# Half of a head's weight transposes go from TensorE to VectorE and DMA, with round-robin buffers and a larger DMA reserve in the order

## The chip, the cores and the metric

The kernel runs on one core of one Trainium2 chip. The core has TensorE (matmuls, PE in the profile), VectorE (DVE), ScalarE (ACT), GpSimd (POOL) and SyncE (SP), whose queue issues every DMA of this kernel. The metric is the device time of one execution in microseconds. Before the change, three runs took 823.62, 824.11 and 825.51 us; the median is 824.11.

## The reference, cut to what matters

One layer of an encoder is computed for a prompt of 1024 positions and a sample of 32 later positions, 1056 rows of 1024 features, in float32. Eight heads of 64 features ("A") do a banded softmax attention with a bias by relative position, eight heads ("B") a stick-breaking attention over all earlier positions.

```python
hn = rmsnorm(h, g_pre)
qa, ka, va, ga, qb, kb, vb, gb = split(hn @ w_in)          # 8 x 512 columns
# A: each chunk of 64 rows reads its own chunk and the 8 before
w = softmax(qa @ ka.T * HD ** -0.5 + bias[rel] , where ok); oa = w @ va
# B: strictly causal
z = qb @ kb.T * HD ** -0.5
w = exp(log_sigmoid(z) + sum of log_sigmoid(-z) over later keys); ob = w @ vb
y = concat(oa * silu(ga), ob * silu(gb)) @ w_out
h = h + rmsnorm(y, g_post)
h = h + sigmoid(h @ w_ple_gate) * (p @ w_ple)
```

The keys and values of both kinds of heads are returned too.

## The kernel before, in words

Every float32 operand of a product is split into a high part, rounded to the format of TensorE's fast float32 product, and the rest (hi and lo); a product is then two or three matmuls.

The work comes in three parts. First x is normalized, transposed and split (tiles `hnh`, `hnl`), while `w_ple` is applied to the first rows. Then come eight pairs of heads, A0, B0, A1, B1 and so on to B3. For each pair the projections of q, k and v (`mm_qA`, `mm_kA`, `mm_vA`, 72 matmuls of 352 columns each) run between the attention of the pair before; with the last pair run the eight gates. Last come the output product and the gate product by a scheme of seven products instead of eight (`o`, `g`).

The attention of one head goes over eight tiles of 128 queries (`attention`, L711). `scores(i)` (L728) makes the scores of tile i: two matmuls into a bank `S`, and for A a VectorE operation that adds the bias and finds the maximum, an exponential on ScalarE into `w1` (tile `be`), a reciprocal, and a scaling on POOL. For B it is two sigmoids on ScalarE, a scan on VectorE and a product on POOL. `weights_t(i)` (L771) then turns the weights: TensorE transposes each block of 128 keys into a bank `ptw`, ScalarE copies the bank into the high part `wTh`, and VectorE subtracts it from the bank for the low part `wTl`. `values(g)` (L798) multiplies the turned weights of four tiles (g = 0 or 1) with V into `PV`, and the head's output goes to DRAM. A tile of A has at most five blocks of keys: 1, 2, 3, 4, 5, 5, 5, 5 for i = 0 to 7. Tile i's transposes are called two tiles behind its scores, and the value products two behind the last tile.

V itself is turned in another way already (`values_out`, L611): VectorE transposes 32 x 32 squares, a DMA writes the result to DRAM (`swapA`), and four DMAs read it back with the squares in their places (`stv`).

The order of all this isn't the order of the calls. The calls only record operations (`Recorder`); `order` (L307) then plans them with a cost for each operation (`cost`, L274) and an order of keys (attention before projections), engine by engine, and issues them so. Each engine, and SP's queue, takes its own list in order. A DMA is taken to land 1500 ns after its issue, plus its bytes at 320 B/ns, plus a reserve `DMA_MARGIN` (L165) of 800 ns. The planner has no cost for ScalarE's table loads.

Buffers have a fixed number of rooms by tag: `om` and `be` (softmax and sigmoid work, and at the start the rows of x and their squares) have three rooms of a full row each; `wTh` and `wTl` have two rooms each of four blocks by 512 queries. A new tile waits for the tile that had the room before.

`g_pre` is spread over 128 partitions by a matmul of a row of ones, one partition deep (L1218 and the lines behind it). The 32 sample rows of V are kept in a tile `vsT`, filled by POOL (`after_v`, L697) and read by `sample_attention` (L840).

Of the kernel before, what the change touches and what calls it, by code (L numbers as in the profile page):

```python
# [13 lines left out]
P = 128  # L14
# [12 lines left out]
NT = 9  # L27

# [127 lines left out]

class Op:
# [7 lines left out]
DMA_NS, DMA_RATE, DMA_MARGIN = 1500, 320.0, 800  # L165
# [3 lines left out]
class Pool:  # L169
# [8 lines left out]
    def tile(self, shape, dtype, tag=None, name=None, bufs=1):  # L178
        b = Buf(shape, dtype, self, tag or name, name, bufs)
        line = self.tags.setdefault(b.tag, [])  # L180
        after = {line[-1].place} if line else {self.opened} if self.opened else set()
        b.place = self.rec.node("CTL", b.take, (), {}, after)
        if len(line) >= bufs:
            self.rec.turns.append((b.place, line[len(line) - bufs]))
        self.ops.append(b.place)
        line.append(b)
        return b
# [12 lines left out]
class Recorder:  # L200
# [43 lines left out]
    def add(self, eng, what, args, kw):  # L244
        writes, reads = [], []
        method = what[1] if isinstance(what, tuple) else ""
        for i, a in enumerate(args):
            if isinstance(a, (View, Raw)):
                (writes if i == 0 or (method == "tensor_tensor_reduce" and i == 7) else reads).append(a)
        for k, a in kw.items():  # L250
            if isinstance(a, (View, Raw)):
                (writes if k in ("out", "accum_out") else reads).append(a)
        o = self.node(eng, what, args, kw, set())
        for mine, write in ((reads, False), (writes, True)):
            for v in mine:
                b = v.buf
                hit = False
                for other, box, wrote in b.uses:
                    if other is not o and (write or wrote) and all(p < y and x < q for (p, q), (x, y) in zip(v.box, box)):
                        o.after.add(other)  # L260
                        hit = True
                if b.pool is not None:
                    if not hit:
                        o.after.add(b.place)
                    b.pool.ops.append(o)
                b.uses.append((o, v.box, write))
        o.busy, o.late = self.cost(eng, method, args, kw, writes, reads)
        o.shared = eng == "POOL"
        if eng == "DVE":
            sbuf = [v for v in reads if isinstance(v, View) and not v.buf.psum and v.free() > 4]  # L270
            o.shared = len(sbuf) > 1 or (method == "tensor_copy" and len(sbuf) == 1 and not writes[0].buf.psum)

    @staticmethod
    def cost(eng, method, args, kw, writes, reads):  # L274
# [3 lines left out]
        psum = any(isinstance(v, View) and v.buf.psum for v in reads)  # L278
# [96 lines left out]
    def emit(self, tc):  # L375
        ops = self.order()
        with tc.manual_schedule():
            for o in ops:
                if o.eng == "CTL":
                    o.what()  # L380
                    continue
                args = [a.get() if isinstance(a, (View, Raw)) else a for a in o.args]
                kw = {k: a.get() if isinstance(a, (View, Raw)) else a for k, a in o.kw.items()}
                if isinstance(o.what, tuple):
                    getattr(getattr(tc.nc, o.what[0]), o.what[1])(*args, **kw)  # L385
                else:
                    o.what(*args)
# [3 lines left out]
def stream_step(  # L391
# [26 lines left out]
    r_dr = scratch([8, 768], "r_dr")  # L418
    ple_dr = scratch([T, D], "ple_dr")
# [25 lines left out]
    vsT = const.tile([NS, 4, P], F32, tag="vsT", name="vsT")  # L445
# [29 lines left out]
    def ensure(j):  # L475
# [6 lines left out]
        if j == 2:  # L482
            pair = [at.tile([P, 2, 4, P], F32R, tag=tag, name=f"{tag}_{kind}{p}", bufs=2) for tag in ("wTh", "wTl")]
# [14 lines left out]
    def load_x(t):  # L498
        n = min(P, T - t * P)
        if t == 3:  # L500
            x34.append(at.tile([P, 2, D], F32, tag="wTh", name="x34", bufs=2))
        xt = x34[0][:, t - 3] if t in (3, 4) else at.tile([P, D], F32, tag="om", name=f"x{t}", bufs=3)
# [9 lines left out]
    def scale_x(t, xt, n, gp):  # L512
        sq = at.tile([P, D], F32, tag="be", name=f"sq{t}", bufs=3)
# [25 lines left out]
    def bias_rows():  # L539

        rb = at.tile([8, 257], F32, tag="om", name="rb", bufs=3)
        dma(rb, rel_bias[0])
        R = at.tile([8, 768], F32, tag="be", name="R", bufs=3)
# [101 lines left out]
    def col_steps(j):  # L645
# [65 lines left out]
    def attention(ab, p, h):  # L711
# [16 lines left out]
        def scores(i):  # L728
# [5 lines left out]
            w0 = at.tile([P, SEQ + 1], F32, tag="om", name=f"om{nm}_{i}", bufs=3)  # L734
            w1 = at.tile([P, SEQ], F32, tag="be", name=f"be{nm}_{i}", bufs=3)
# [31 lines left out]
            state[i] = w1  # L767

        wT = {}

        def weights_t(i):  # L771
            g, q = i // 4, (i % 4) * P
            for j in range(i // 4 + 1):
                if (g, j) not in wT:
                    wT[g, j] = [at.tile([P, 4, 4 * P], F32R, tag=tag, name=f"{tag}{nm}_{g}_{j}", bufs=2) for tag in ("wTh", "wTl")]
            b0 = lo_block(i)
            w1 = state.pop(i)
            b = b0
            while b <= i:
                j = b // 4  # L780
                e = min(i + 1, 4 * (j + 1))
                m = e - b
                pt = psum("T", f"ptw{nm}_{i}_{j}")
                for x in range(m):
                    nc.tensor.transpose(pt[:, x * P:(x + 1) * P], w1[:, (b - b0 + x) * P:(b - b0 + x + 1) * P], ident)
                hi, lo = wT[g, j]
                o = b - 4 * j
                src = pt[:, 0:m * P].rearrange("p (b c) -> p b c", b=m)
                nc.scalar.copy(hi[:, o:o + m, q:q + P], src)
                nc.vector.tensor_tensor(lo[:, o:o + m, q:q + P], src, f(hi[:, o:o + m, q:q + P]), ALU.subtract)  # L790
                b = e
# [6 lines left out]
        def values(g):  # L798
# [41 lines left out]
    def sample_attention(ab, gi):  # L840
# [9 lines left out]
        def load():  # L850
            Kc = at.tile([P, 4, 256], F32, tag="be", name="Kc" + nm, bufs=3)
# [34 lines left out]
        def scores():  # L886
# [6 lines left out]
            w0 = at.tile([P, SEQ + 1], F32, tag="om", name="w0" + nm, bufs=3)  # L893
            w1 = at.tile([P, SEQ], F32, tag="be", name="w1" + nm, bufs=3)
# [22 lines left out]
            Vc = at.tile([P, 4, 256], F32, tag="be", name="Vc" + nm, bufs=3)  # L917
            dma(Vc, cv[0, 0, :, h4, :].rearrange("(b p) h d -> p b (h d)", p=P))
            bx["Vc"] = Vc

        def weights():
# [24 lines left out]
            for a in range(2):  # L946
                new, c = vsT[:, at_[a], :], slice(a * P, (a + 1) * P)
                nc.vector.tensor_copy(vh4[0:NS, c], new)
                nc.vector.tensor_tensor(vl4[0:NS, c], new, f(vh4[0:NS, c]), ALU.subtract)
# [273 lines left out]
    nc.vector.tensor_copy(ghl[:, 0], grow)  # L1223
    nc.vector.tensor_tensor(ghl[:, 1], grow, f(ghl[:, 0]), ALU.subtract)
# [513 lines left out]
```

## Time and profile before

| | |
|---|---|
| median of 3 runs | 824.11 us |
| the profiled execution | 822.94 us |
| its span, first to last instruction | 821.2 us |
| TensorE, matmuls busy | 806.5 us |
| VectorE busy | 588.7 us |
| ScalarE busy | 536.5 us |
| POOL busy | 498.6 us |
| moved by DMA | 135.57 MB |

The profile is one execution with every instruction's start and length. Names are out<-in by the program's tiles, with the numbers of buffers left out and the pair left out, so `wThA<-ptwA` is the copy of turned weights of any head of A. Every operation is issued from one line of the recorder (L385), so groups are told apart by tile. A row of the groups has the busy time of the group, the mean length of one in ns, and the idle time of the engine before them with what ended it. Matmuls are pipelined: the busy time counts a matmul to its modelled end, and the next has begun by then.

### The profile page before, as it was taken

What the parts mean: (1) busy time and instruction counts of PE and PEld (TensorE: products, weight loads), DVE (VectorE), ACT (ScalarE), POOL (GpSimd) and SP (SyncE); (2) the same over time, 40 slices, a digit from 0 to 9 for tenths busy, and PEclk for the clock granted to TensorE, in tenths of its full rate; (3) what the DMA queues carried; (4) which work ended last, traced back from release to release, by engine and by line L of the source; (5) the groups of instructions that cost most, each with busy time, mean ns of one, the idle gap of its engine ahead of it and who ended that gap; (6) DMA issues with size and microseconds to landing.
All of it is one profiled execution on the core that took longest, in us unless ns stands there. A gap on an engine that the chain in (4) does not pass through costs nothing.

```text
span 821.2 us, 14722 instructions
## 1 busy us (share of the span) xinstructions
PE 806.5 (98%) x4814; PEld 742.7 (90%) x4814; DVE 588.7 (72%) x1165; ACT 536.5 (65%) x1179; POOL 498.6 (61%) x559
## 2 busy tenths in 40 slices
PE   9999999999999999999999999999999999999997
PEld 7999999999999998999999998999998787888786
DVE  5717588987687898687887787983664676686755
ACT  4735588776476667687685676653437866886741
POOL 5625785996676959554753454675462527599613
PEclk9999999999999999999999999999999999999999
DMA  8419854526764545633413544253489847749733
GB/s 296 122 39 277 208 178 149 142 60 203 214 178 155 152 135 153 154 91 88 97 40 98 139 122 145 74 160 112 134 264 291 293 142 242 252 153 361 248 117 128
DMA packets 137855, 135.57 MB, mean 165 GB/s; under 512 B 36450, under 2 KB 103818, under 8 KB 137779
## 3 DMA queue, kind: packets, MB, share of 16 engines
q1 hardware_dynamic: 137778, 134.64, 55.0%
q8 instruction: 38, 0.62, 0.3%
q14 instruction: 39, 0.31, 0.2%
HBM read 85.41 MB, written 40.79 MB: 154 GB/s over the span
## 4 chain that ended last, share of the span: by engine, by line
PE 83%; DVE 6%; ACT 4%; DMA 4%; issue 2%; SPq 0%; POOL 0%; DVEq 0%; ACTq 0%
PE mm_gB L385 5%; PE mm_qA L385 5%; PE mm_kB L385 5%; PE mm_kA L385 5%; PE mm_vA L385 4%; PE mm_vB L385 4%; PE mm_qB L385 4%; PE PVB L385 4%; PE SB L385 3%; PE ple L385 3%; PE PVA L385 3%; PE mm_gA L385 3%; PE ptwB L385 3%; PE ptwA L385 3%; PE SA L385 3%; PE g1P L385 2%
## 5 line engine op out<-in xcount | busy, mean ns | idle before, releaser
L385 POOL TENSOR_TENSOR beB<-beB,omB 128x128 f32<-128x128 f32 (+7 forms) x64 | 87.2, 1364 | 75.3 <-ACT beB L385 31.5
L385 DVE TENSOR_TENSOR_SCAN omB<-omB 128x128 f32<-128x128 f32 (+7 forms) x64 | 106.5, 1675 | 6.6 <-POOL omB L385 3.5
L385 POOL TENSOR_SCALAR beA<-beA,statA 128x640 f32<-128x640 f32 (+2 forms) x64 | 48.2, 755 | 50.1 <-DVE statA L385 47.9
L385 DVE TENSOR_TENSOR wTlA<-ptwA,wThA 128x128 fp32r<-128x128 f32 (+3 forms) x96 | 45.5, 483 | 27.8 <-ACT wThA L385 27.0
L385 ACT CAST wThA<-ptwA 128x128 fp32r<-128x128 f32 (+3 forms) x96 | 39.7, 422 | 32.1 <-PE ptwA L385 30.5
L385 ACT ACTIVATE omB<-SB 128x384 f32<-128x384 f32 (+5 forms) x96 | 47.1, 501 | 14.7 <-DVE SB L385 8.3
L385 DVE TENSOR_TENSOR wTlB<-ptwB,wThB 128x512 fp32r<-128x512 f32 (+3 forms) x96 | 50.7, 545 | 8.1 <-ACT wThB L385 7.2
L385 ACT CAST wThB<-ptwB 128x512 fp32r<-128x512 f32 (+3 forms) x96 | 44.7, 485 | 16.9 <-PE ptwB L385 16.3
L385 ACT ACTIVATE beA<-omA,statA 128x640 f32<-128x640 f32 (+2 forms) x64 | 44.7, 700 | 7.2 <-DVE statA L385 5.6
L385 ACT ACTIVATE beB<-SB 128x384 f32<-128x384 f32 (+5 forms) x96 | 45.4, 500 | 6.0 <-PE ptwB L385 3.2
L385 PE MATMUL ptwB<-ident,beB 128*128 128x128 f32 x288 | 44.9, 274 | 0.1
L385 PE MATMUL ptwA<-ident,beA 128*128 128x128 f32 x240 | 40.2, 274 | 0.8 <-POOL beA L385 0.8
L385 PEld LDWEIGHTS ptwB<-ident,beB 128*128 128x128 f32 x288 | 34.9, 140 | 3.4 <-DVE wTlB L385 0.8
L385 POOL TENSOR_TENSOR gB<-gB,gB 128x256 f32<-128x256 f32 x32 | 29.1, 929 | 13.8 <-issue 7.4
L385 PE MATMUL SB<-kdB,LB 128*128 128x384 f32 (+5 forms) x96 | 34.6, 364 | 0.3 <-ACT beB L385 0.2
L385 POOL TENSOR_TENSOR oB<-oB,oB 128x256 f32<-128x256 f32 x32 | 28.4, 903 | 8.6 <-DMA oB<-in_w_out_dram 4.6
L385 PE MATMUL SB<-klB,LB 128*128 128x384 f32 (+5 forms) x96 | 33.1, 346 | 0.0
L385 DVE CUSTOM_DVE_ANT_0 omA<-SA,biasA 128x320 f32<-128x320 f32 (+2 forms) x64 | 30.7, 479 | 3.2 <-PE SA L385 1.9
L385 PEld LDWEIGHTS ptwA<-ident,beA 128*128 128x128 f32 x240 | 30.2, 140 | 2.7 <-POOL beA L385 1.1
L385 PE MATMUL SA<-kdA,LA 128*128 128x320 f32 (+2 forms) x96 | 30.5, 327 | 1.4 <-DVE LA L385 1.2
L385 PE MATMUL SA<-klA,LA 128*128 128x320 f32 (+2 forms) x96 | 29.9, 321 | 0.0
L385 POOL TENSOR_TENSOR h<-h,x 128x512 f32<-128x512 f32 (+1 forms) x18 | 23.3, 1321 | 0.8 <-DVE h L385 0.8
(712 smaller groups left out, 2674.5 us busy)
## 6 DMA issues: line engine op xcount, KB each, us to landing
x<-in_x_prompt_dram SPq DMA_DIRECT2D x8, 512.0 KB, 5.9
oB<-in_w_out_dram SPq DMA_DIRECT2D x16, 256.0 KB, 4.0
sum_dro<-oB SPq DMA_DIRECT2D x16, 256.0 KB, 2.3
gB<-in_w_ple_gate_dram SPq DMA_DIRECT2D x16, 256.0 KB, 3.8
sum_drg<-gB SPq DMA_DIRECT2D x16, 256.0 KB, 2.8
x<-in_x_prompt_dram SPq DMA_DIRECT2D x16, 256.0 KB, 3.7
h_dr<-h SPq DMA_DIRECT2D x8, 512.0 KB, 3.5
ht<-h_dr SPq DMA_DIRECT2D x8, 512.0 KB, 5.5
```

Of the source, the lines that this page charges most:

```text
L385: getattr(getattr(tc.nc, o.what[0]), o.what[1])(*args, **kw)
```

## The change

There are five parts.

1. The turning of the weights of A's tiles 0, 2, 4 and 6 (`swapped`). VectorE transposes 32 x 32 squares of `w1` into the tile's other work tile `w0`, grouped by target; a DMA writes `w0` to DRAM, four DMAs (one for each 32 partitions) read it back into `w1`, ScalarE copies `w1` into the high part and VectorE subtracts the high part from `w1` for the low part. TensorE and the bank `ptw` aren't used for these tiles. The other tiles of A and all of B stay on TensorE, now in groups of four blocks from the tile's first block.
2. Round-robin rooms (`Arena`): `om`, `be`, `wTh` and `wTl` are one tile each, of 3076, 3384, 4224 and 4224 columns, from which pieces of the size needed are handed out in turn, starting over at the end; a piece waits for all pieces that lay where it lies. The turned weights lie one query tile behind the other, and the value product reads them through an access pattern with a step (`Segments`).
3. The planner's reserve on a DMA's landing is 2000 ns instead of 800.
4. `g_pre`: the ones are 128 x 128 and the row stands in the first of 128 rows, the others cleared by VectorE.
5. The sample's rows of V go by DMA to DRAM and come back with the cached values, in place of the copies on POOL.

```diff
+def swapped(ab, p, h, i):
+    return ab == "A" and i % 2 == 0
...
-DMA_NS, DMA_RATE, DMA_MARGIN = 1500, 320.0, 800
+DMA_NS, DMA_RATE, DMA_MARGIN = 1500, 320.0, 2000
...
+class Segments:
+    def __init__(self, buf, start, step, n):
+        self.buf, self.start, self.step, self.n = buf, start, step, n
...
+    def get(self):
+        base = self.buf.get()[:, self.start:self.start + P]
+        return bass.AP(tensor=base.tensor, offset=base.offset, ap=[base.ap[0], [self.step, self.n], [1, P]])
...
+class Arena:
...
+    def tile(self, shape, name, dtype=None):
...
+        size = -(-n // 8) * 8
+        if self.at + size > self.cols:
+            self.at = 0
+        lo, hi = self.at, self.at + size
+        self.at = hi
...
+        for c, d, x in self.live:
+            if c < hi and lo < d:
+                old.append(x)
...
+        b.place = self.rec.node("CTL", take, (), {}, {self.whole.place} | {x.place for x in old})
+        for x in old:
+            self.rec.turns.append((b.place, x))
...
+    ring0, ring1 = Arena(rec, at, "om", 3076), Arena(rec, at, "be", 3384)
+    ringh, ringl = (Arena(rec, at, x, 33 * P, F32R) for x in ("wTh", "wTl"))
...
-            nc.gpsimd.tensor_scalar(vsT[:, slot(ab, p), :], tok[0:NS, 8, :], 1.0, 1.0, ALU.mult, ALU.mult)
+            dma(vs_dr[ab][:, p * P:(p + 1) * P], tok[0:NS, 8, :])
...
-            w0 = at.tile([P, SEQ + 1], F32, tag="om", name=f"om{nm}_{i}", bufs=3)
-            w1 = at.tile([P, SEQ], F32, tag="be", name=f"be{nm}_{i}", bufs=3)
+            w0 = ring0.tile([P, n + (ab == "B")], f"om{nm}_{i}")
+            w1 = ring1.tile([P, n], f"be{nm}_{i}")
...
+        LAID = {("A", 0): (3, 13), ("A", 1): (4, 20), ("B", 0): (3, 13), ("B", 1): (7, 29)}
...
+            if swapped(ab, p, h, i):
+                nc.vector.transpose(w0[:, 0:n * P].rearrange("p (c b q) -> p b c q", c=4, q=32), w1)
+                dr = scratch([P, n * P], f"swap{nm}_{i}")
+                dma(dr, w0[:, 0:n * P])
+                for c in range(4):
+                    x = dr[:, c * n * 32:(c + 1) * n * 32].rearrange("(g k) x -> k g x", k=32)
+                    dma(w1[32 * c:32 * c + 32].rearrange("k (g x) -> k g x", g=4), x)
+                src = w1.rearrange("p (g b q) -> p g b q", g=4, q=32)
+                hi, lo = (x.rearrange("p (b g q) -> p g b q", g=4, q=32) for x in (hi, lo))
+                nc.scalar.copy(hi, src)
+                nc.vector.tensor_tensor(lo, src, f(hi), ALU.subtract)
+                return
+            for b in range(0, n, 4):
...
+                nc.scalar.copy(hi[:, c], pt[:, 0:m * P])
+                nc.vector.tensor_tensor(lo[:, c], pt[:, 0:m * P], f(hi[:, c]), ALU.subtract)
...
-                nc.tensor.matmul(acc[:, c], v2[:, b, :], wT[g, j][half][:, b - 4 * j, c], start=(n == 0), stop=(n == len(todo) - 1))
+                step = LAID[ab, g][0]
+                w = Segments(wT[g][half], c.start * step + b * P, step * P, (c.stop - c.start) // P)
+                nc.tensor.matmul(acc[:, c], v2[:, b, :], w, start=(n == 0), stop=(n == len(todo) - 1))
...
-    ones = at.tile([1, P], F32R, tag="ot", name="ones", bufs=3)
+    ones = at.tile([P, P], F32R, tag="ot", name="ones", bufs=3)
...
-    ghl = at.tile([1, 2, D], F32R, tag="wTl", name="ghl", bufs=2)
+    ghl = ringl.tile([P, 2, D], "ghl")
+    for part in range(2):
+        nc.vector.memset(f(ghl[:, part]), 0.0)
```

More of the change, by code (lines that the diff above doesn't have):

```diff
@@ L269, in add @@
         if eng == "DVE":
-            sbuf = [v for v in reads if isinstance(v, View) and not v.buf.psum and v.free() > 4]
+            sbuf = [v for v in reads if isinstance(v, (View, Segments)) and not v.buf.psum and v.free() > 4]
             o.shared = len(sbuf) > 1 or (method == "tensor_copy" and len(sbuf) == 1 and not writes[0].buf.psum)
@@ L277, in cost @@
         n = out.free() if isinstance(out, View) else 1
-        psum = any(isinstance(v, View) and v.buf.psum for v in reads)
+        psum = any(isinstance(v, (View, Segments)) and v.buf.psum for v in reads)
         if eng == "PE":
@@ L482, in ensure @@
         if j == 2:
-            pair = [at.tile([P, 2, 4, P], F32R, tag=tag, name=f"{tag}_{kind}{p}", bufs=2) for tag in ("wTh", "wTl")]
+            pair = [ringl.tile([P, 2, 4, P], f"w{x}_{kind}{p}") for x in "hl"]
         for kh in range(2):
@@ L766, in scores @@
                 nc.gpsimd.tensor_scalar(w1[:, 0:n], w1[:, 0:n], m[:, 3:4], 1.0, ALU.mult, ALU.mult)
-            state[i] = w1
+            state[i] = w0, w1
         wT = {}
+        LAID = {("A", 0): (3, 13), ("A", 1): (4, 20), ("B", 0): (3, 13), ("B", 1): (7, 29)}
         def weights_t(i):
[L772 to L775, printed above, removed]
+            g = i // 4
+            step, size = LAID[ab, g]
+            if g not in wT:
+                wT[g] = [x.tile([P, size * P], f"{x.name}{nm}_{g}") for x in (ringh, ringl)]
@@ L776, in weights_t @@
             b0 = lo_block(i)
[L777 to L783, printed above, removed]
-                for x in range(m):
[L785 to L791, printed above, removed]
+            w0, w1 = state.pop(i)
```

79 lines of the change are left out of this document (58 added, 21 removed).

## The prediction

> **What bounds the kernel.** I read the page's busy shares first, then its chain, then what TensorE waited for, and last the stretches in which the heads of A run.
>
> ```profile
> span 821.2 us, 14722 instructions
> PE 806.5 (98%) x4814; PEld 742.7 (90%) x4814; DVE 588.7 (72%) x1165; ACT 536.5 (65%) x1179; POOL 498.6 (61%) x559
> PE 83%; DVE 6%; ACT 4%; DMA 4%; issue 2%; SPq 0%; POOL 0%; DVEq 0%; ACTq 0%
> ```
> ```profile
> PE PVB L385 <- DVE v2B L385: 1.8, 1, 1.8
> ...
> PE PVA L385 <- ACT wThA L385: 1.2, 1, 1.2
> ...
> PE ptwA L385 <- POOL beA L385: 0.8, 1, 0.8
> ...
> PE PVA L385 <- DVE v2A L385: 0.6, 1, 0.6
> ```
>
> TensorE is busy for 98% of the span and makes up 83% of the chain. The second fence is TensorE's list of waits behind its first microseconds (total, times, longest): no wait reaches 2 us. So work taken from TensorE shortens the kernel unless it comes back as a wait. The question is whether the order, fixed at build time, still always has a matmul ready.
>
> ```profile
> core 0: us, PE busy (x) PEld busy (x) DVE busy (x) ACT busy (x) POOL busy (x), PEclk, DMA share, GB/s
> 64.00:124.00 60.00, 57.32 (x375) 55.09 (x374) 43.75 (x125) 40.25 (x95) 41.40 (x53) 1.00 0.80 219
> ...
> 185.00:248.00 63.00, 61.61 (x406) 59.22 (x406) 47.16 (x143) 40.18 (x98) 44.13 (x59) 1.00 0.69 196
> 248.00:312.00 64.00, 63.48 (x418) 61.16 (x417) 55.87 (x88) 45.48 (x105) 46.03 (x51) 1.00 0.50 145
> 312.00:368.00 56.00, 55.38 (x362) 52.69 (x361) 40.92 (x124) 41.21 (x98) 37.66 (x43) 1.00 0.51 136
> ...
> 435.00:492.00 57.00, 56.81 (x384) 55.17 (x383) 44.14 (x140) 39.38 (x95) 25.13 (x33) 1.00 0.49 128
> ```
>
> These are the four stretches of the A pairs (64, 185, 312 and 435 us) and one B pair (248 us). VectorE is at 73 to 79% in the A stretches and at 87% in the B stretch, where TensorE still works 63.48 of 64 us. Hence VectorE at 87% is not yet a bound. The first A stretch also has the DMA engines at 0.80.
>
> **The transposes that go.** Tiles 0, 2, 4 and 6 of a head of A have 1, 3, 5 and 5 blocks of keys, 14 for a head and 112 for eight heads, of the 240 below. The built order agrees: 4814 matmuls become 4702.
>
> ```profile
> 330.30 0.49 PE L385 MATMUL mm_kB<-hnl,wh_kB 128*128 128x352 f32 x2
> 330.63 0.60 PE L385 MATMUL ptwA<-ident,beA 128*128 128x128 f32 x4
> 330.98 0.41 PE L385 MATMUL mm_kB<-hnl,wh_kB 128*128 128x352 f32 x1
> 331.23 0.22 PE L385 MATMUL SA<-kdA,LA 128*128 128x128 f32 x1
> ```
> ```profile
> L385 PE MATMUL ptwA<-ident,beA 128*128 128x128 f32 x240 | 40.2, 274 | 0.8 <-POOL beA L385 0.8
> ```
>
> In the timeline (start, length) two projections take 0.33 us, 0.165 each. Four transposes take 0.35, and the projection behind them takes 0.25 instead of 0.165. That is 0.44 for four, 0.11 each, and 112 x 0.11 = 12.3 us. The bounds are 112 x 0.35/4 = 9.8 (no delay behind them) and 112 x 40.2/240 = 18.8 (the group's busy time, which includes drains that overlap other matmuls). I take 12.3, because matmul starts measure what follows and busy time doesn't.
>
> **What takes their place.** A swapped tile costs one square transpose on VectorE, one DMA out, four DMAs back, one ScalarE copy and one VectorE subtraction, both now from SBUF.
>
> ```profile
> L385 DVE STREAM_TRANSPOSE vxA<-stvA 128x1024 f32<-128x1024 f32 x4 | 5.0, 1240 | 0.4 <-ACT stvA L385 0.4
> ...
> L385 DVE STREAM_TRANSPOSE ktA<-stkA 128x512 f32<-128x512 f32 x4 | 2.8, 703 | 11.8 <-ACT stkA L385 11.8
> ```
> ```profile
> L385 DVE TENSOR_TENSOR wTlA<-ptwA,wThA 128x512 fp32r<-128x512 f32 x24 | 16.5, 688 | 10.9 <-ACT wThA L385 10.6
> ...
> L385 DVE TENSOR_TENSOR oT<-woT,oT 128x512 fp32r<-128x512 f32 x8 | 7.6, 966 | 1.2 <-ACT oT L385 1.2
> ...
> L385 DVE TENSOR_TENSOR oB<-woB,oB 128x512 fp32r<-128x512 f32 x8 | 6.8, 854 | 7.0 <-ACT oB L385 7.0
> ...
> L385 DVE TENSOR_TENSOR wTlA<-ptwA,wThA 128x128 fp32r<-128x128 f32 x24 | 6.7, 279 | 0.2
> ```
>
> The two square transposes give 166 ns + 1.05 ns a column, so 0.30, 0.57, 0.84 and 0.84 us for a head: 20.4 us for eight. The subtraction from PSUM goes from 279 (128 columns) to 688 (512); with both inputs in SBUF, 512 columns take 854 to 966, some 1.32 times as long. Six subtractions a head (half of the 45.5 us of the whole group) become four: (0.28 + 0.55 + 0.82 + 0.82) x 1.32 x 8 = 26 against 22.7 us. VectorE gains about 24 us, 6 for each A pair: the 64 us stretch goes from 43.75 to some 50 of 60, 83%, still below the B stretch. I cost it at nothing; without that cover it is bounded by 24 us. ScalarE's copies change from six to four a head, by one us or two in all. On POOL eight small copies of V go.
>
> ```profile
> swapA<-vxA SPq DMA_DIRECT2D x4, 512.0 KB, 2.6
> stvA<-swapA SPq DMA_DIRECT2D x16, 128.0 KB, 3.4
> ...
> o_dr<-otA SPq DMA_DIRECT2D x32, 64.0 KB, 2.2
> ...
> out_dram<-ktA SPq DMA_DIRECT2D x16, 64.0 KB, 3.2
> ```
> ```profile
> L385 SPq DMA_DIRECT2D stvA<-swapA x16: 303/423/464, 78.3 to 438.5; - x16
> ...
> DMA to landing us min/median/max: 2.6/3.4/7.0
> ```
>
> SP's queue gets 160 DMAs for the tiles and 12 for V of the sample (608 become 780). At 0.42 us an issue that is 72 us over 440, and it lies beside TensorE. Each tile crosses two landings in a row: 2.6 + 3.4, four issues, a copy and a subtraction, about 9 us from square to operand. Everything behind a swap in SP's queue stands when the queue waits for the square or for the first landing: weight loads, output rows, the doubled keys. The data is 1792 columns x 128 x 4 B = 0.92 MB each way for a head, 3.67 MB a pair, 61 GB/s in a stretch. In the first A stretch 219 + 61 = 280 stands against 219/0.80 = 274 GB/s: 2% of 60 us, between 0 and 1.3 us; I take 0.7. The other stretches have room.
>
> **Waits that the new order brings.** I counted in both built orders, behind the first 60 us, the places where TensorE has no matmul left between the start of a producer on another engine and the matmul that needs it. There are 13 before and 38 after; 13 of the 38 are value products of A that stand directly behind the copy of a swapped tile. The four waits listed above, 1.8 + 1.2 + 0.8 + 0.6 = 4.4 us, are what such places cost before, 0.34 each. The 25 new ones cost between 0 and 25 x 0.34 = 8.5 us. I take the middle, 4.2: the planner now reserves 1.5 + 1.0 + 2.0 us for 320 KB out, while 512 KB landed in 2.6, so half of these producers should be early.
>
> ```profile
> 117.25 0.75 ACT L385 CAST wThA<-ptwA 128x384 fp32r<-128x384 f32 x2
> 118.02 1.28 ACT L385 ACT_TABLE_LOAD   x1
> 119.31 0.28 ACT L385 ACTIVATE omB<-SB 128x128 f32<-128x128 f32 x1
> ```
> ```profile
> 313.90:317.90 4.00, 3.44 (x20) 1.00 0.40 90
> ...
> sum 28.00, PE 27.13; mean PE 3.88
> ```
>
> ScalarE's table loads go from 8 to 18 in the built order: where A hands over to B, late exponentials of A now stand between early sigmoids of B, and the planner's costs have no term for it. Ten loads x 1.28 = 12.8 us of ScalarE. The second fence is TensorE in the four microseconds behind each of the seven old loads between heads: it lost 0.87 us in all. So ten more cost 1.2 us by that rate, 12.8 if all lies on the path; I take 1.5, because they come in pairs. [...]
>
> **The rest.** The rooms change which tile waits for which; no row prices that, and it is counted in the 25 places. The reserve moves consumers of every DMA later in the order; that can take away waits such as the 1.8 us on v2B, which stands behind a DMA round trip, so its gain is bounded by 1.8 + 0.6.
>
> ```profile
> 0.87 0.38 DVE L385 MEMSET newh<- 128x384 f32 x1 [0.87 <-PEq L1726]
> ...
> 2.18 0.81 DVE L385 CAST ghl<-grow 1x1024 fp32r<-1x1024 f32 x1 [0.93 <-DMA grow<-in_g_pre_dram]
> ...
> 3.02 1.21 DVE L385 TENSOR_TENSOR ghl<-grow,ghl 1x1024 fp32r<-1x1024 f32 x1
> ...
> 5.92 2.07 PE L385 MATMUL gpre<-ghl,ones 1*128 1x512 f32 x4
> ```
>
> g_pre on 128 rows adds two clears of 1024 columns, 0.38 x 1024/384 = 1.0 us each, ahead of the copy: 1.25 + 2.0 + 0.81 + 1.21 = 5.3 us, before the matmul at 5.92. It costs nothing.
>
> **Sum.** The profiled execution took 822.94 us, 1.2 below the median 824.11. 822.94 - 12.3 + 4.2 + 1.5 + 0.7 = 817.0, and on the median's scale 818.2: I predict 818.
>
> **The rivals.**
> - Everything is covered. The swapped tiles are early everywhere, the loads hide, and late landings of V stop: 824.1 - 12.3 - 2 = 810. For it: 0.87 us lost behind seven loads; against it: 13 value products with nothing in front of them.
> - The chain of a swapped tile comes late, and TensorE, which takes its queue in order, stands at A's value products. It decides from 12.3/13 = 0.95 us each. The 1.8 us on v2B is just such a square with a DMA round trip; at 1.8 each, 824.1 - 12.3 + 23.4 = 835. For it speaks a landing of 7.0 us among medians of 3.4, and that 64 KB in packets of 128 B (ktA) took 3.2 us where packets of 1 KB (otA) took 2.2: the swapped reads have packets of 128 to 640 B. [...]
> - ScalarE's loads fall on the path at the hand-overs: 824.1 - 12.3 + 12.8 + 4.2 = 829. Against it: the old loads.
> - The change doesn't do what it says: the attention chain sets the pace and the freed 12.3 us turn into idle TensorE. 822.5 to 825.8. Against it: the shares of the other engines.
>
> **Chances.** 818 (812.5 to 822.4) has 0.45, all covered 0.15, late chains 0.22, loads on the path 0.10, no change 0.08. A measurement tells 0.2%, 1.6 us, from no change. So faster has 0.60, same 0.08, slower 0.32. For 8 in 10 the range reaches from 809 (12.3 and the late landings gone, and a little more busy time than starts show) to 832, which takes in the loads and most late chains.
>
> **What would show it.** ptwA x128 and about 27 us busy; TensorE busy near 794; 48 square transposes, of which 32 near 0.3 to 0.84 us; 18 table loads. The four stretches of A shorter by 2 to 3 us each shows the sum right. In TensorE's waits, PVA behind ACT wTh in more than ten places of under 0.5 us shows the 4.2 right; over 0.95 us, the second rival. If waits sit at the hand-overs behind loads, it is the third. The forecast is wrong if SP's queue makes the weights late, which would show as projections waiting for wh or wl.

## The result and the profile after

The changed kernel takes 830.10 us (median of 13 runs, 825.94 to 831.01), the kernel before 823.17 us in runs beside it (13 runs, 819.42 to 826.20). The ratio is 1.0079 with a 95% interval of 1.0059 to 1.0098. By the ratio it is 6.5 us slower, where 6 us faster was predicted. The profiled execution took 828.38 us.

The busy shares and the chain of the page of the changed kernel:

```profile
span 826.4 us, 14790 instructions
PE 796.8 (96%) x4702; PEld 729.9 (88%) x4702; DVE 604.0 (73%) x1175; ACT 547.6 (66%) x1173; POOL 506.6 (61%) x551
PE 73%; DMA 9%; ACT 6%; POOL 4%; SPq 3%; DVE 3%; issue 2%; ACTq 0%; POOLq 0%; DVEq 0%
```

TensorE works 9.7 us less than before, and the span is 5.2 us longer. Its idle time has doubled, from 821.2 - 806.5 = 14.7 to 826.4 - 796.8 = 29.6 us. In the chain TensorE falls from 83 to 73%; DMA comes to 9% from 4, and SP's queue, nothing before, to 3%.

The same five stretches by the clock (start and end, length, busy time and count for each engine, granted clock, DMA share, GB/s):

```profile
64.00:124.00 60.00, 55.06 (x344) 51.81 (x343) 44.56 (x124) 40.62 (x87) 35.66 (x46) 1.00 0.86 244
185.00:248.00 63.00, 58.40 (x371) 55.78 (x370) 46.06 (x131) 37.27 (x84) 34.31 (x43) 0.97 0.76 212
248.00:312.00 64.00, 62.45 (x408) 59.95 (x407) 57.59 (x92) 51.13 (x114) 47.55 (x57) 1.00 0.59 166
312.00:368.00 56.00, 53.61 (x346) 51.32 (x345) 42.43 (x128) 35.82 (x81) 38.20 (x46) 1.00 0.74 194
435.00:492.00 57.00, 54.87 (x356) 52.49 (x354) 42.87 (x131) 36.02 (x79) 23.05 (x28) 1.00 0.55 145
```

Most of the loss is in the four A stretches: TensorE is idle there for 14.1 of 236 us, where it was 4.9 before, which is 9.2 of the 14.9 us of added idle time. VectorE is hardly fuller in the first two (44.56 and 46.06, before 43.75 and 47.16), because the work moves slower. In the second stretch the granted clock was 0.97.

TensorE's waits in the changed kernel (total, times, longest):

```profile
PE PVA L453 <- ACT wTh L453: 3.5, 5, 1.1
PE PVsA L453 <- DVE Vh0sA L453: 3.5, 1, 3.5
PE ptwA L453 <- POOL be L453: 3.2, 3, 1.7
PE SB L453 <- ACT be L453: 1.9, 2, 1.7
PE SA L453 <- DVE statA L453: 1.7, 2, 0.9
...
PE mm_vB L453 <- ACT wh_vB L453: 0.3, 1, 0.3
```

Value products behind the copy of a weight tile are there, as feared. But none of the four next to them is at a swapped tile's operands; the longest single one is the sample's attention, which waits for cached values (`Vh0sA`) that come by a DMA of their own.

The moved work, in groups (count, busy time, mean ns, idle before and what ended it) and as DMA issues (count, KB each, median us to landing):

```profile
L453 PE MATMUL ptwA<-ident,be 128*128 128x128 f32 x128 | 21.5, 282 | 3.9 <-POOL be L453 3.2 <-POOL om L453 0.6
L453 DVE STREAM_TRANSPOSE om<-be 128x640 f32<-128x640 f32 x16 | 13.4, 839 | 1.7 <-POOL be L453 1.4
L453 ACT CAST wTh<-be 128x640 fp32r<-128x640 f32 x16 | 11.7, 730 | 11.1 <-DMA be<-swapA 11.1
L453 DVE TENSOR_TENSOR wTl<-be,wTh 128x640 fp32r<-128x640 f32 x16 | 14.6, 920 | 3.2 <-ACT wTh L453 3.1
L453 ACT ACT_TABLE_LOAD x18 | 23.1, 1283 | 3.5 <-issue 1.3 <-DVE statA L453 1.2 <-PEq L1815 0.7
swapA<-om SPq DMA_DIRECT2D x16, 320.0 KB, 4.1
be<-swapA SPq DMA_DIRECT2D x64, 80.0 KB, 2.8
DMA packets 161470, 150.52 MB, mean 182 GB/s; under 512 B 47393, under 2 KB 125385, under 8 KB 161394
```

The instructions are as forecast: 112 transposes gone, square transposes of 0.84 us, 18 table loads. The 128 transposes left are busy for 21.5 us and not for the 27 forecast: that figure took the 12.3 us, which are counted by starts, off the 40.2 us of busy time. New is that ScalarE stands 11.1 us before the copies of the large swapped tiles, waiting for their landing.

### The profile page after: what moved, and what is told of

It reads as the page before. It is cut to its first block, busy times and chain, and to the rows that moved or that the text cites. A ratio compares the mean times of both kernels' runs of the same rounds, so it can differ in the third digit from the quotient of the medians.

```text
span 826.4 us, 14790 instructions
## 1 busy us (share of the span) xinstructions
PE 796.8 (96%) x4702; PEld 729.9 (88%) x4702; DVE 604.0 (73%) x1175; ACT 547.6 (66%) x1173; POOL 506.6 (61%) x551
## 4 chain that ended last, share of the span: by engine, by line
PE 73%; DMA 9%; ACT 6%; POOL 4%; SPq 3%; DVE 3%; issue 2%; ACTq 0%; POOLq 0%; DVEq 0%
PE mm_gB L453 5%; PE mm_qA L453 5%; PE mm_vA L453 5%; PE mm_gA L453 4%; PE mm_kB L453 4%; PE PVB L453 4%; PE ptwB L453 4%; PE mm_kA L453 4%; SPq L453 3%; PE SB L453 3%; PE mm_qB L453 3%; PE g0P L453 2%; PE g1P L453 2%; PE o1P L453 2%; PE o3P L453 2%; PE o0P L453 2%
## 5 line engine op out<-in xcount | busy, mean ns | idle before, releaser
L453 POOL TENSOR_TENSOR be<-be,om 128x256 f32<-128x256 f32 (+8 forms) x66 | 91.2, 1391 | 48.9 <-DVE om L453 22.6
L453 DVE TENSOR_TENSOR_SCAN om<-om 128x256 f32<-128x256 f32 (+8 forms) x66 | 110.8, 1688 | 4.5 <-ACT om L453 3.7
L453 POOL TENSOR_SCALAR be<-be,statA 128x640 f32<-128x640 f32 (+2 forms) x64 | 47.1, 741 | 67.1 <-DVE statA L453 38.3
L453 ACT CAST wTh<-ptwB 128x512 fp32r<-128x512 f32 (+3 forms) x96 | 44.1, 484 | 22.7 <-PE ptwB L453 21.4
L453 ACT ACTIVATE be<-om,statA 128x640 f32<-128x640 f32 (+3 forms) x64 | 44.5, 696 | 18.4 <-DVE statA L453 14.6
L453 DVE TENSOR_TENSOR wTl<-ptwB,wTh 128x512 fp32r<-128x512 f32 (+3 forms) x96 | 50.0, 542 | 7.9 <-ACT wTh L453 7.7
L453 ACT ACTIVATE om<-SB 128x384 f32<-128x384 f32 (+5 forms) x96 | 47.1, 503 | 5.3 <-DVE SB L453 4.4
L453 ACT ACTIVATE be<-SB 128x384 f32<-128x384 f32 (+5 forms) x96 | 45.4, 500 | 4.1 <-DVE Vl2sB L453 2.6
L453 PE MATMUL ptwB<-ident,be 128*128 128x128 f32 x288 | 44.6, 273 | 0.1
L453 PEld LDWEIGHTS ptwB<-ident,be 128*128 128x128 f32 x288 | 35.1, 140 | 2.4 <-POOL be L453 0.7
```

## The experiments

Every ratio is to the kernel before, run beside it on the same chip, with its 95% interval. One percent is 8.2 us.

### The change without the swap

```diff
-    return ab == "A" and i % 2 == 0
+    return False
```

> The changed kernel with no tile swapped: all 240 transposes of A stay on TensorE, the rooms, the reserve of 2000 ns, g_pre and the sample's V stay as changed. Theory R (the round trip of the swapped tiles makes the waits): the other parts cost nothing, the built order has 8 places where TensorE has no matmul in front of it against 13 before and 38 with the swaps, at 0.43 us each about 2 us less than the kernel before: 819 to 823 us. Theory P (the new rooms or the larger reserve make a worse order): the waits stay and 12 us of transposes come back on top of the changed kernel, 835 to 842 us.

Measured: 814.72 us, 0.9932 [0.9913, 0.9951], below the ranges of both theories. Rooms, reserve, g_pre and the sample's V together make the kernel 5.6 us faster, so the swap costs (1.0079 - 0.9932) x 823 = 12 us, though it takes 12.3 us of matmuls away: some 24 us come back. By the two pages TensorE's idle time grew by 18.4 us (29.6 with the swap, 812.1 - 800.9 = 11.2 without), while 112 matmuls fewer took only 800.9 - 796.8 = 4.1 us off its busy time. Together with the run without the swap at the smaller reserve (below, 0.9934) this is the fastest kernel found that computes the reference; it beats both.

```profile
64.00:124.00 60.00, 58.80 (x386) 56.94 (x386) 45.68 (x131) 45.83 (x108) 41.82 (x54) 1.00 0.72 198
185.00:248.00 63.00, 62.47 (x421) 60.50 (x420) 50.98 (x133) 42.46 (x101) 43.46 (x59) 1.00 0.66 191
```

These are its first two A stretches. TensorE works 58.80 and 62.47 us in them, against 55.06 and 58.40 with the swap.

### Without the round trip

```diff
-                dr = scratch([P, n * P], f"swap{nm}_{i}")
-                dma(dr, w0[:, 0:n * P])
-                for c in range(4):
...
-                src = w1.rearrange("p (g b q) -> p g b q", g=4, q=32)
+                src = w0[:, 0:n * P].rearrange("p (g b q) -> p g b q", g=4, q=32)
```

> Swapped tiles keep the square transpose on VectorE, the copy on ScalarE and the subtraction on VectorE, but the DMA out and the four DMAs back are left out, so the squares stay in their partitions and the turned weights of these tiles are not the right ones. Theory R: the 29 places without a matmul in front go (9 are left of 38) and the gain of the transposes shows: 815 to 819 us. Theory V (VectorE's 24 us more, or its subtraction with two inputs in SBUF holding POOL back, make the waits): 826 to 831 us, as the whole change.

Measured: 807.85 us, 0.9847 [0.9824, 0.9870], faster than either theory had it. With the square transposes, the copies and the subtractions in place (`wTl<-om,wTh`, 968 ns for 640 columns), the kernel is 19 us faster than the changed one. So VectorE's added work and the slower subtraction cost little, at most the 5 us by which the gain on the run without the swap, 7.0 us, falls short of 12.3; the round trip through DRAM costs the rest. POOL did work slower beside the swapped tiles' subtractions: in the changed kernel two of its products of 128 x 256 (`oB`), begun at 130.1 and 131.4 us beside the subtractions of 129.8 to 132.2, take 1.32 us each, where the median of all 32 is 0.74.

### The table loads kept at eight

```diff
                 for a, b, s in pieces:
                     nc.scalar.activation(w0[:, a:b], s, AF.Sigmoid, scale=-1.0)
+                    of_set("B")
...
                 nc.scalar.activation(w1[:, 0:n], w0[:, 0:n], AF.Exp, bias=m[:, 2:3], accum_out=m[:, 3:4])
+                of_set("A")
```

(`of_set` puts each activation behind all those of the other kind recorded ahead of it.)

> The whole change, and in the recorded order no sigmoid of B may stand before the last exponential of the head of A ahead of it, nor the other way round: table loads 8 instead of 18, everything else planned anew. Theory T (the ten added table loads make the waits at the hand-overs from A to B, 9.4 us in the trace of the changed kernel): 820 to 822 us. Theory R: the late last tiles of A keep TensorE waiting all the same, and B's start now waits for them: 32 places instead of 38, 826 to 831 us.

Measured: 829.75 us, 1.0113 [1.0090, 1.0136]. Ten loads fewer make nothing faster, though in an order with a constraint of its own, which could hide a small gain. The run without the trip's DMAs, further below, settles it: with all 18 loads, in the order of the changed kernel, it takes 812.47 us. The loads fall as a cause.

### Only tile 4

```diff
-    return ab == "A" and i % 2 == 0
+    return ab == "A" and i == 4
```

> Only tile 4 of each head of A is swapped, 40 transposes instead of 112. Theory R (each swapped tile holds its two rooms for the round trip, and one in a head finds cover): 9 places without a matmul in front, 40 x 0.11 = 4.4 us of TensorE saved, 815 to 819 us. Theory P or V: waits in proportion to the tiles, 8 of 32 swapped, so 823 to 826 us.

Measured: 822.48 us, 1.0024 [1.0005, 1.0043], between the two ranges. A quarter of the DMAs (40) already takes back (1.0024 - 0.9932) x 823 = 7.6 us against the kernel without the swap, although 40 x 0.11 = 4.4 us of transposes go. The cost isn't in proportion to the number of swapped tiles. Each kernel has an order of its own here, and I can't say what of this is the order. The later runs remove that doubt for the whole change; for this kernel it stays.

### The traffic beside, and the rooms

In the first of these two kernels all DMAs are issued but the operands come from `w0`; in the second the reads back go to DRAM as well, so that `w1` is free early.

```diff
-                src = w1.rearrange("p (g b q) -> p g b q", g=4, q=32)
+                src = w0[:, 0:n * P].rearrange("p (g b q) -> p g b q", g=4, q=32)
```
```diff
-                dr = scratch([P, n * P], f"swap{nm}_{i}")
+                dr, back = (scratch([P, n * P], f"{x}{nm}_{i}") for x in ("swap", "back"))
...
-                    dma(w1[32 * c:32 * c + 32].rearrange("k (g x) -> k g x", g=4), x)
+                    dma(back[32 * c:32 * c + 32].rearrange("k (g x) -> k g x", g=4), x)
```

> All 160 DMAs of the swapped tiles are issued as in the whole change, with the same rooms and bytes, but ScalarE and VectorE take the squares from the tile that the DMA out reads, so no operand waits for a landing (the turned weights of these tiles are the squares left in their partitions). Theory R1 (operands behind two landings make the waits): 807 to 812 us beside 820 for the kernel before, as without the round trip. Theory R2 (the two rooms of each swapped tile are held until the landings, and later tiles of the head start late): 820 to 828 us, near the whole change.

> As the run with the trip beside, but the four DMAs back write to DRAM instead of the tile's first room, which is free after the square transpose; 160 DMAs and their bytes stay, operands don't wait for a landing. Theory R2 (rooms): nearer to 808 than the run before it, 809 to 816 us. Theory Q (the 160 DMAs in SP's queue and on the DMA engines delay weights, keys and V): no better than the run before it, 820 us or more.

Measured: 822.85 us, 1.0007 [0.9990, 1.0023], and 830.65 us, 1.0105 [1.0080, 1.0129]. Traffic that nobody waits for costs 13 us against the kernel without the trip. The first run lies in the range of R2 (rooms), the second refutes it: freeing the rooms early doesn't help, it costs 8 us more. Only Q allows that (820 us or more), without a reason for it. The lengths of the issues in SP's queue suggest one (minimum, median and maximum ns), first of the second kernel, then of the first:

```profile
L453 SPq DMA_DIRECT2D backA<-swapA x128: 519/598/1401, 82.3 to 507.6; - x128
```
```profile
L453 SPq DMA_DIRECT2D be<-swapA x128: 302/432/2029, 82.0 to 497.1; - x128
```

Here a DMA from DRAM to DRAM took SP 0.60 us to issue, one from DRAM to SBUF 0.43 (medians). By them the second kernel holds SP's queue for 128 x 0.17 = 21 us more; added up over the traces, the trip's 160 issues take 95 against 78 us, 17 more. That was only a suspicion at this point.

### The reserve, with and without the swap

```diff
-DMA_NS, DMA_RATE, DMA_MARGIN = 1500, 320.0, 2000
+DMA_NS, DMA_RATE, DMA_MARGIN = 1500, 320.0, 800
```

> The whole change with the planner's reserve on a landing at 800 ns as before. Theory L (swapped tiles land later than planned, so engines stand in order before them): 830 to 840 us beside 820, as with less reserve more landings are late. Theory R2 (the order has nothing to put in the gaps, 37 places against 38): within 3 us of the whole change, 824 to 830 us.

> No tile swapped and the reserve at 800 ns: of the change only the rooms, g_pre and the sample's V are left. The run without swaps was 5.6 us faster than the kernel before. If the rooms bring that, 814 to 816 us; if the reserve brings it, 819 to 821 us (13 places without a matmul in front, as in the kernel before, against 8 with the larger reserve, 2 us at 0.43 each).

Measured: 836.89 us, 1.0164 [1.0131, 1.0197] for the whole change at 800; 817.12 us, 0.9934 [0.9913, 0.9955] without the swap at 800. Without the swap the reserve is worth nothing (0.9932 and 0.9934), so the 5.5 us come from the rooms (with g_pre and the sample's V, which weren't run apart). With the swap the step from 800 to 2000 saves 7 us.

### One order, with the trip taken apart

From here on every engine keeps exactly the order of the changed kernel; the operations are planned as they were, and only what is issued in their places differs. (The four reads and the subtraction are treated as the write and the copy shown.) `put` replaces an operation's operands behind the planning. The added lines below are alternatives: the first with the last makes the run without DMAs, the last alone the one with all bytes, the second alone the slivers that are waited for, the second with the last those that aren't, and the third with the last the free issues further below.

```diff
                 dma(dr, w0[:, 0:n * P])
+                rec.ops[-1].put = ()                               # no DMA
+                rec.ops[-1].put = dr[:, 0:8], w0[:, 0:8]           # or a sliver
+                rec.ops[-1].put = dr[0:16, 0:8], x_sample[0, 0:16, 0:8]   # or free of waits
...
                 nc.scalar.copy(hi, src)
+                rec.ops[-1].put = hi, here                         # no wait: the identity
```

> The changed kernel with every engine's instructions in exactly its order, but the five DMAs of each swapped tile aren't issued and the copy and the subtraction read a constant tile (the identity) in place of w1, so that nothing waits for a landing; the turned weights of the 32 swapped tiles are therefore not the true ones. Order, square transposes, copies and subtractions all stay. O (the order that the planner makes for the swapped tiles is what costs, whatever its DMAs do): within 4 us of the changed kernel, ratio to before 1.003 to 1.010. Every theory that puts the cost on the DMAs: ratio 0.983 to 0.990 (808 to 814 us), as in the run whose order was planned without the round trip.

> The changed kernel in exactly its order with all its DMAs, but the copy and the subtraction of a swapped tile read the identity, so they don't wait for the landing (their operands are not the true weights). W (waiting for the landing at the operands is the cost): as without the DMAs, ratio 0.983 to 0.990. Q (five more DMAs a tile in SP's queue) or B (their bytes and small packets on the DMA engines): ratio 0.998 to 1.008. The run with an order of its own gave 1.0007.

> The changed kernel in exactly its order, all 160 DMAs issued and waited for, but each moves only 8 columns (4 KB out, 1 KB back in place of 64 to 320 KB and 16 to 80 KB), so the turned weights of swapped tiles are not the true ones. B (bytes and packets): ratio 0.985 to 0.993. Q (issues and waits in SP's queue): ratio 1.003 to 1.009. W (the time from square to operand): the two landings of some 3 to 4 us shrink to about 2 each but don't vanish, so in between, 0.995 to 1.004, with ACT's wTh still waiting for be.

> As the run before (8 columns a DMA, the same order), and the copy and the subtraction read the identity and wait for no landing: only the 160 issues and their places in SP's queue are left (operands not the true weights). Q: ratio 0.998 to 1.008, as with the full bytes. B or W: as without the DMAs, 0.983 to 0.990.

| in the order of the changed kernel | ratio | median us |
|---|---|---|
| no DMA of the trip, no wait | 0.9869 [0.9817, 0.9920] | 812.47 |
| 160 slivers, no wait | 0.9969 [0.9940, 0.9997] | 821.31 |
| 160 slivers, landings waited for | 1.0017 [0.9990, 1.0044] | 824.97 |
| all bytes, no wait | 1.0047 [1.0020, 1.0073] | 826.67 |
| all bytes, landings waited for (the change) | 1.0079 [1.0059, 1.0098] | 830.10 |

The order is hardly at fault: without the DMAs it runs nearly as fast as the order that was planned without them (0.9847). Issues alone, with next to no bytes and no operand waiting (SP itself still waits for each square), cost 0.0100 x 823 = 8.2 us. The bytes cost 6.4 us without waits and 5.1 with them. Waiting at the operands costs 4.0 us with slivers and 2.6 with all bytes. No single theory had that: Q (the queue), B (bytes) and W (waits) each hold a part. Each step is uncertain by 3 to 5 us; the last alone is not told from nothing.

As the matmuls come in one order, the traces can be laid over each other, matmul by matmul. The changed kernel loses 16.2 us against the one without DMAs, and seven places make 13.8 of it: 5.3 at `PVsA` (232 us), 2.4 at `SB` and at `PVA` behind it (108 to 111), 2.0 at `ptwA` (356), and 0.6 to 1.2 at four more, all in the A stretches or within 30 us behind them. The largest, in SP's queue: first the kernel without DMAs of the trip, then the changed one (start, length, operation, count).

```profile
212.50 0.95 SPq L465 DMA_DIRECT2D wr_vB<-in_w_in_dram  x2
213.50 0.49 SPq L465 DMA_DIRECT2D oB<-in_w_out_dram  x1
214.09 0.38 SPq L465 DMA_DIRECT2D gB<-in_w_ple_gate_dram  x1
214.53 0.42 SPq L465 DMA_DIRECT2D biasA<-r_dr  x1
215.00 0.42 SPq L465 DMA_DIRECT2D be<-in_cache_a_v_dram  x1
```
```profile
217.68 1.86 SPq L453 DMA_DIRECT2D be<-swapA  x4
...
220.42 0.94 SPq L453 DMA_DIRECT2D wr_vB<-in_w_in_dram  x2
221.41 0.50 SPq L453 DMA_DIRECT2D be<-swapA  x1
221.96 0.43 SPq L453 DMA_DIRECT2D oB<-in_w_out_dram  x1
222.43 0.43 SPq L453 DMA_DIRECT2D gB<-in_w_ple_gate_dram  x1
222.91 1.39 SPq L453 DMA_DIRECT2D be<-swapA  x3
224.40 0.38 SPq L453 DMA_DIRECT2D biasA<-r_dr  x1
224.87 0.40 SPq L453 DMA_DIRECT2D be<-in_cache_a_v_dram  x1
```

From 220 us on SP issues one DMA behind the other without a pause; the load of the cached values goes out 9.9 us later than without the trip, while the matmuls around it are 4.8 us late. In the changed kernel VectorE and TensorE then stand for it:

```profile
231.16 0.85 DVE L453 CAST Vh0sA<-be 128x512 fp32r<-128x512 f32 x1 [1.03 <-DMA be<-in_cache_a_v_dram]
```
```profile
232.16 0.35 PE L453 MATMUL PVsA<-Vh0sA,whsA 128*128 128x256 f32 x1 [3.47 <-DVE Vh0sA L453]
```

Over the first A stretch (60 to 130 us) the other DMAs are issued later against the matmuls by a median of 2.5 us in the changed kernel and 2.7 with slivers that nobody waits for; in the later A stretches by 0.2 to 0.7 in either, with a tenth of them over 2 to 5 us late; in the B stretches by 0.0.

### Issues without waits, and a larger reserve

```diff
-DMA_NS, DMA_RATE, DMA_MARGIN = 1500, 320.0, 2000
+DMA_NS, DMA_RATE, DMA_MARGIN = 1500, 320.0, 3500
```

> The changed kernel in exactly its order; each of the 160 DMAs of the swapped tiles copies 16 x 8 elements from an input to DRAM, so it waits for no engine and for no landing of another of them, and the copy and the subtraction read the identity (operands not the true weights). Left are 160 issues in their places in SP's queue, each with its turn among the eight semaphores that SP's DMAs take in rotation. I (the time of the issues themselves, 160 x about 0.42 us, where SP's queue is full): as with slivers that wait, ratio 0.995 to 1.000. H (SP stands at the head of its queue for a square or for a landing, and everything behind it stands too): as without the DMAs, 0.984 to 0.990.

> The whole changed kernel, the planner's reserve on a landing 3500 ns in place of 2000. L (landings come later than the order was built for, so that engines stand before them): faster than the changed kernel by half or more of what the step from 800 to 2000 gave (7 us), 822 to 827 us, ratio 0.999 to 1.004. S (the queue itself sets when the loads are issued, and no reserve changes that): within 2 us of the changed kernel, 1.005 to 1.011.

Measured: 830.68 us, 1.0096 [1.0064, 1.0128], and 844.56 us, 1.0298 [1.0225, 1.0371]. Both are misses, and the first is the telling one. Its DMAs wait for no engine and for no landing of the trip, and it is 10 us slower than the slivers, whose DMAs wait for both. The lengths of its issues, and then those of the slivers:

```profile
L465 SPq DMA_DIRECT2D swapA<-in_x_sample_dram x160: 488/587/1447, 72.8 to 507.6; - x160
```
```profile
L465 SPq DMA_DIRECT2D be<-swapA x128: 303/420/1559, 84.1 to 493.9; - x128
L465 SPq DMA_DIRECT2D swapA<-om x32: 319/408/1444, 72.0 to 483.6; - x32
```

Added up over the traces, the trip's issues hold SP for 97 us here and for 77 us there: 20 us more of issuing, 10.5 us more of time. The two kernels with traffic beside stand alike: 17 us more of issuing, 8 us of time. Ahead of the trip's DMAs SP stands idle for 13.4 us with the slivers and for 1.2 us with the free issues. So the loss needs no standing at the head of the queue (H); the time that issuing takes is enough. Whether the 13.4 us of standing cost something besides is not shown. The DMA engines are not the reason: the landing of the DRAM copies hardly differs (a median of 2.2 us against 2.0), and the engines are no fuller, as the first A stretch shows with slivers and then with free issues (share next to last):

```profile
64.00:124.00 60.00, 56.30 (x358) 54.29 (x358) 46.32 (x125) 42.59 (x93) 36.86 (x48) 1.00 0.72 197
```
```profile
64.00:124.00 60.00, 56.22 (x356) 53.74 (x355) 46.03 (x124) 41.38 (x90) 35.67 (x47) 1.00 0.71 193
```

The larger reserve doesn't take the lateness back. It makes the kernel 18 us slower than the change, with TensorE idle for 37.3 us. Both theories had it within 2 us of the change, or faster. That 2000 is better than 800 and than 3500 with the swap is measured; why 3500 costs so much is open. (Some 6 of the 18 us can be the granted clock, a mean of 0.988 in these runs against 0.995 with the change.) Issuing the trip from another engine's queue wasn't tried, nor a place for the cached values that is free earlier.

## Why the prediction was wrong, step by step

**The step that failed** is the one on SP's queue: "At 0.42 us an issue that is 72 us over 440, and it lies beside TensorE." The size was about right: 128 x 0.430 + 32 x 0.388 = 67 us by the medians of these rows of the changed kernel, 78 us when all the lengths are added up.

```profile
L453 SPq DMA_DIRECT2D be<-swapA x128: 302/430/1797, 82.8 to 504.3; - x128
L453 SPq DMA_DIRECT2D swapA<-om x32: 319/388/1282, 72.2 to 494.1; - x32
```

The cover was wrong, because I spread it over 440 us. All of it falls between 72 and 127, 188 and 254, 321 and 379, and 439 and 504 us, 244 us together, where SP had its other loads to issue too. Added up over the traces, the issues that begin in the four A stretches listed above took 102 of their 236 us before and take 165 now; in the first it is 32 and 49 of 60. There the queue runs without a pause for several us at a time, and loads behind come late. I had written that everything behind a swap stands when the queue *waits*, and priced that at nothing; in fact it needs no wait. The price of issuing is 8 us.

**The bytes** were put at 0.7 us, from the mean rate of the first stretch (280 against 274 GB/s). Measured, the stretch moved 244 GB/s at a share of 0.86, and the bytes cost 5 to 6 us. A landing also took 4.1 us for 320 KB, where I took 2.6 from another tile. How the bytes cost so much is not shown: the 6.4 us appear with no operand behind those landings, and in that run the other DMAs land no later in the first stretch than without the trip, in the second (185 to 255 us) after a mean of 4.2 us instead of 3.6.

**The waits of the new order** were put at 4.2 us, the middle between 0 and 8.5. By the starts of the matmuls, the 38 places without a matmul in front hold 16.5 us of idle time, the 13 before held 5.7: 10.8 more, above the upper bound. (All of TensorE's idle time behind the first 60 us grew from 7.9 to 21.8 us.) Each costs 0.43 in both kernels; the four waits listed on the page, from which I took 0.34 and which I multiplied for the new places alone, didn't show all of them. What makes producers late there is mostly the two points above, so this is the same time seen from TensorE and not a term to add to them.

**The rooms and the reserve** weren't priced, and the reserve was bounded by 2.4 us. The rooms, with g_pre and the sample's V, gave 5.5 us, the only gain among the parts that stands by itself. The reserve gave 0 without the swap and 7 with it.

**Right were** the transposes (in the order of the changed kernel without its DMAs, six of them start 0.11 us apart, and the kernel without the trip is 7.0 us faster than the one without the swap, which leaves 5 us of the 12.3 lost to waits: TensorE is idle for 806.1 - 789.9 = 16.2 us against 11.2); VectorE and the slower subtraction at nothing, or next to it; and the table loads at hardly anything, as the run without the trip's DMAs shows with all 18.

As a sum: -5.6 (rooms and the rest), -7.0 (squares in place of transposes, all waits but the trip's), +1.8 (an order planned for the trip), +8.2 (its issues), +6.4 (its bytes), +2.6 (its landings) = +6.4, beside the 6.5 measured. Each term is the step between two neighbouring ratios, so the sum has to come out and proves nothing by that; each of the last four is uncertain by 3 to 5 us.

**The rivals.** The late chain of a swapped tile (835 us) had the place half right: `PVA` waits behind `wTh` in five places for 3.5 us together, 0.7 each, below the 0.95 from which it decides. The third, table loads, falls. I named the right sign to look for, "if SP's queue makes the weights late", but with the wrong victim: TensorE's waits show only 0.3 us on a projection's weights (`wh_vB`), but 3.5 on the cached values (`PVsA`), where the run without the trip's DMAs has none. The waits at the banks of the scores (`SA` behind `statA`, `SB` behind `be`, 1.7 and 1.9 us) aren't of the queue's making: they are 1.8 each in that run too.

I should have weighed that SP, which issues every DMA of this kernel, can itself set when loads come: from 220.42 to 225.27 us in the changed kernel its issues fill 4.47 of 4.85 us, at a share of 0.73 of the DMA engines.

## What to carry to other kernels

Price an added DMA by the time of its issue in the stretch where it is issued, against what the same queue must issue there, not over the whole kernel: here 77 us of issuing, in stretches of which issuing took 43% already, cost 8 us, and the next 17 to 20 cost 8 to 10. In this kernel one to five transposes of 0.11 us on TensorE weren't worth the five DMAs of 0.4 us that replaced them. To find out what of a trip costs, keep the order and empty the trip, rather than plan anew without it.

## What the runs showed of the hardware

The wait of 3.47 us at `PVsA` cost 5.3, because TensorE ran slowly behind it. Stretches of the changed kernel before, in and behind the wait (granted clock third from the right):

```profile
225.00:228.00 3.00, 2.95 (x21) 2.63 (x20) 1.50 (x7) 0.68 (x2) 2.58 (x4) 1.00 0.74 178
228.00:232.00 4.00, 0.68 (x5) 0.38 (x3) 1.85 (x5) 3.44 (x8) 1.70 (x4) 1.00 0.71 236
232.80:236.20 3.40, 3.40 (x16) 3.33 (x15) 2.23 (x8) 0.40 (x2) 0.80 (x1) 0.52 0.68 204
236.20:240.00 3.80, 3.80 (x29) 3.80 (x28) 3.16 (x9) 3.69 (x7) 1.99 (x1) 1.00 0.26 56
```

For 3.4 us the granted clock is at half and 16 matmuls run where 26 would at the rate behind it; half of the 3.4 us, 1.7, is my estimate of what such a stretch can cost. In the changed kernel the clock is at half for 3.41 us, from 232.65 to 236.06; with all bytes and no wait for 6.8, from 231.6 to 238.4, and that begins within the wait of 4.6 us at `PVsA`. The length of the wait alone doesn't tell. With slivers that are waited for, 1.87 us at `PVA` has 3.41 us at half behind it (first fence: the wait, then the stretch behind it); with slivers that nobody waits for, 3.06 us at `PVsA` has none (second fence). What sets the clock is not shown.

```profile
108.99:110.86 1.87, 0.00 (x0) 0.00 (x0) 0.14 (x3) 0.78 (x2) 0.54 (x1) 1.00 0.52 142
110.91:114.32 3.41, 3.41 (x12) 3.22 (x13) 3.00 (x9) 3.34 (x6) 2.23 (x2) 0.50 0.40 123
```
```profile
224.90:228.00 3.10, 0.04 (x2) 0.03 (x1) 0.78 (x2) 0.92 (x2) 1.70 (x4) 1.00 0.34 109
228.00:231.40 3.40, 3.40 (x25) 3.38 (x26) 3.26 (x11) 1.29 (x3) 0.80 (x1) 1.00 0.48 156
```

So in these runs the wait of 1.87 us came with up to 1.7 us of lost clock, and the one of 4.6 with up to 2.2 (half of the 4.4 us at half clock left behind it), beyond what the waits show; both are estimates from the half clock, and this is part of the prices above. The two kernels with traffic beside had two such stretches and five in their profiled executions (clocks of 0.995 and 0.989), and mean clocks of 0.994 and 0.986 over all their runs: at most 6 of the 8 us between them. Between the slivers without waits (0.994) and the free issues (0.993) it is about 1 of 10.

The length of an issue differed with where the DMA went: medians of 0.59 to 0.60 us from DRAM to DRAM, 0.42 to 0.43 from DRAM to SBUF, with DMAs of the same shapes in the two kernels with traffic beside.
